# Feed-forward up projections with 512-column passes over both operand parts, one PSUM bank per output block

## The chip, the cores and the metric

The kernel runs on one core of one Trainium2 chip. The metric is the device time of one execution in microseconds (us); lower is better. TensorE does the matrix products, VectorE (DVE in the profile) and ScalarE (ACT) do the elementwise work, SyncE (SP) issues the loads, GpSimd (POOL) does almost nothing here.

## What is computed

Two layers of an encoder block over 256 tokens of 1024 features, all in float32. Each layer is a half-step feed-forward, a mixer (a state-space branch called S5, attention, and a convolution branch, gated and merged), and a second half-step feed-forward. The change touches the feed-forwards, of which there are four in all:

```python
D_MODEL, SEQ, DEPTH, D_FF = 1024, 256, 2, 2816

def rmsnorm(x, g):
    return x * lax.rsqrt(jnp.mean(x * x, axis=-1, keepdims=True) + EPS) * g

def swiglu_ffn(x, w_up, w_down):            # w_up: 1024 x 5632, w_down: 2816 x 1024
    a, b = jnp.split(x @ w_up, 2, axis=-1)
    return (jax.nn.silu(a) * b) @ w_down

def reference(...):
    for l in range(DEPTH):
        x = x + 0.5 * swiglu_ffn(rmsnorm(x, ffn1_norm[l]), ffn1_w_up[l], ffn1_w_down[l])
        ...                                  # mixer: w_in, three branches, gates, w_out
        x = x + 0.5 * swiglu_ffn(rmsnorm(x, ffn2_norm[l]), ffn2_w_up[l], ffn2_w_down[l])
    return x
```

## The kernel before

The residual stream is kept with features on partitions: `x[128, 8, 256]` is 8 blocks of 128 features by 256 tokens. A weight matrix is cut into 128x128 tiles, and `plan` fixes the order in which the tiles are used. Eight tiles make a chunk of 512 KB, which is one load (`fetch`, lines 318 to 341). For accuracy, each float32 operand is split into a high part and a remainder: for a chunk, ScalarE casts `raw` to `hi` (line 336) and VectorE subtracts to get `lo` (line 337). There are three `raw` and four `hi` and `lo` buffers. The activations are split in the same way, into `xh` and `xl`, which lie side by side in one tile `x2[128, 8, 2, 256]` (`norm_start`, `norm_block`). A product then needs three terms: hi·xh, hi·xl and lo·xh.

`prod` (lines 352 to 374) issues them in one of two forms. Where the operand is given as a pair `(xh, xl)`, a weight tile costs three matmuls of 256 columns, all summed into one 256-column area (lines 371 to 374). Where it is given as one tile that holds both parts, a weight tile costs one matmul of 512 columns, hi over (xh, xl), and one of 256 columns, lo over xh (lines 360 to 370); the two halves of the 512-column output are then added when they leave PSUM. In the kernel before, the down projections use the second form (their operand is `a2`, called AB in the profile) and the up projections and the mixer's projections use the first.

`ffn` (lines 464 to 520) is the feed-forward. The loop over `i` (22 steps) computes two output blocks, the a side and the b side, of 8 weight tiles each: 16 tiles a step. Both blocks of a step share one PSUM bank (line 482), except for the first steps. Then a chain leaves PSUM (lines 488 to 494): DVE multiplies the a side by the token factor `rb`, ACT takes a tanh, DVE multiplies twice (the second time by the b side, straight from PSUM), ACT casts the high part of `a2` and DVE subtracts the low part. After the loop, 8 down blocks of 22 weight tiles each follow; their evacuation `evac` copies one half of the bank with ACT, adds the other half with DVE, and updates `x`. A feed-forward thus has 352 up tiles and 176 down tiles; the four have 1408 up tiles. In the first feed-forward of a layer, `fill` holds the S5 branch's tables, small DVE and ACT work, recorded at the lowest priority (rank 4, line 496). The S5 tables of the second layer run mostly during the second feed-forward of the first layer, ahead of where the code records them.

The order of instructions on each engine is not the order of the code. `Recorder` records all operations with their dependencies, and `schedule` (lines 217 to 262) is a list scheduler that picks an order from rough costs of its own, given by `price` (lines 193 to 215): a float32r matmul of n columns is planned at n/2400 + 0.0025 us. `MARGIN` and `AUX_MARGIN` (0.3 and 0.8 us) are added before a matmul that depends on another engine. Each engine then executes its list strictly in that order, so an instruction that waits holds up all that is queued behind it. All recorded operations have line 268 in the profile, so the groups are told apart by tile names.

PSUM has 8 banks: `mm` has 3, `at` 2, and `y`, `pq` and `ax` 1 each (line 96). `pq` and `y` serve the S5 branch, `ax` the sums of the norms. Tiles of one tag take turns.

Of the kernel before, what the change touches and what calls it, by code (L numbers as in the profile page):

```python
"""Two layers of a parallel-branch encoder block (SwiGLU / S5 + attention + conv mixer / SwiGLU).

The residual stream is kept feature-major: x[feature on partitions, feature block, token].
Every large product runs on the tensor engine in float32r: both operands are split exactly
into a high part of 12 significant bits and the remainder, and three products carry the sum.
RMSNorm's 1/rms factor is per token and linear, so it is applied where a product leaves PSUM.
"""
# [20 lines left out]
EPS = 1e-6  # L28
NH, HD = 8, 64
CW = 31  # L30
U0, Q0, K0, V0, Z0, G0 = 0, 2, 6, 10, 14, 18     # 128-column blocks of w_in
CHT = 8                                            # weight tiles per DMA
MAGIC = 12582912.0                                 # 1.5 * 2**23: adding it rounds to integers
TWO_PI = 6.283185307179586
C1 = float(np.float32(6.28125))                    # 2*pi in three parts
# [13 lines left out]
GLU = 4                                            # blocks of the convolution's branch ahead of S5's GLU  # L49


def plan():
    out = []
    for l in range(L):
        for f in ("ffn1", "ffn2"):
            o = []
            if not out:
                o += [(f + "_w_up", k, c) for k in range(KD) for c in (0, KF, 1, KF + 1)]
            for i in range(2 if not out else 0, KF):
                o += _cols(f + "_w_up", KD, (i, KF + i))  # L60
            # the last operand block as late as possible
            o += _cols(f + "_w_down", KF - 1, (0, 1)) + [(f + "_w_down", KF - 1, c) for c in (0, 1)]
            o += _cols(f + "_w_down", KF, range(2, KD))
            if f == "ffn1":
                o += _cols("w_in", KD, (U0, U0 + 1, Z0, Z0 + 2, Z0 + 1, Z0 + 3))
                for c0 in (Q0, K0, V0):
                    o += [("w_in", k, c0 + c) for k in range(KD) for c in range(4)]
                o += _cols("w_in", KD, range(G0, G0 + 24))
                o += _cols("w_br_attn", 4, range(KD))
                o += _cols("w_br_conv", 2, range(GLU))  # L70
                o += _cols("s5_w_glu", 2, (0, 2, 1, 3))
                o += _cols("w_br_conv", 2, range(GLU, KD))
                o += _cols("w_br_s5", 2, range(KD))
                o += _cols("w_out", KD, range(KD))
            out += [(l,) + t for t in o]
    return out


NATIVE = ("w_br_conv", "s5_w_glu", "w_br_s5")      # few columns: float32 products, operands not split
# [15 lines left out]
TMP = dict(ev=4, th=3, sq=2, sa=2, sc=2, mc=4, s=2, pt=1, cv=2, jk=2)  # L95
# [4 lines left out]
#  # L100
# The program is first recorded in its logical order. Each engine runs its instructions in the order
# of issue, so that order is then chosen by a list scheduler with rough costs (they depend on shapes
# alone): the weight stream and what frees PSUM go first, the mixer's branches fill in.
# [23 lines left out]
class Recorder:  # L127
# [65 lines left out]
    def price(eng, name, outs, ins, kw):  # L193
# [5 lines left out]
        if eng == "pe":  # L199
            if name == "transpose":  # L200
                return 0.112, 0.2
            slow = kw["rhs"].dtype != F32R or n < 256
            rows = outs[0].partition_size()            # tiles of 32 or 64 columns run side by side
            return max(n / 2400.0 * (4 * rows / P if slow else 1) + 0.0025, 0.03), 0.2
# [12 lines left out]
    def schedule(self):  # L217
# [4 lines left out]
        wait = {e: [] for e in engs}       # (ready time, seq, op)  # L222
        can = {e: [] for e in engs}        # (rank, seq, op)
# [6 lines left out]
        while left:  # L230
# [11 lines left out]
            if soon:                       # a short chain that others wait for: no long one in between  # L242
                free[e] = min(soon)
                continue
# [26 lines left out]
# blocks of x that are loaded ahead of a part (chunk, column) of the weights  # L271
# [8 lines left out]
class Builder:  # L280
# [15 lines left out]
    # -- small helpers --  # L296
# [4 lines left out]
    # Tiles of one tag take turns in their slots, so work that runs at its own pace has its own tags.  # L301
# [15 lines left out]
    # -- weight stream --  # L317
# [33 lines left out]
    # -- products: out[feature, token] += w.T @ x --  # L351
    def prod(self, out, keys, ops, ks, start, stop):
        nc = self.nc
        for n, k in enumerate(ks):
# [5 lines left out]
            if not isinstance(ops, tuple):  # L360
                # one pass over both parts; the halves of out are added where it leaves PSUM
# [18 lines left out]
    def quad(self, outs, l, name, cs, ops, nk):  # L380
        """Output blocks that share every operand block as it arrives."""
        for k in range(nk):
            for o, c in zip(outs, cs):
                self.block(o, l, name, c, ops, nk, k, k + 1)

    def pair(self, outs, l, name, cs, ops, nk):
        """Two output blocks whose last operand block is used as late as possible."""
        for o, c in zip(outs, cs):
            self.block(o, l, name, c, ops, nk, 0, nk - 1)
        for o, c in zip(outs, cs):  # L390
            self.block(o, l, name, c, ops, nk, nk - 1, nk)

    # -- 1/sqrt on a small tile: bit-level seed and three Newton steps --
# [12 lines left out]
    def col_rsqrt(self, terms, inv_n, eps=EPS):  # L406
        """terms: [feature, token] tiles whose squares' sums over all features give the variance."""
# [10 lines left out]
    def spread(self, rc, out):  # L418
        """out[:, token] = rc[token] on every partition."""
# [9 lines left out]
    # -- RMSNorm: operands x*g split in two, 1/rms per token --  # L429
# [33 lines left out]
    # -- SwiGLU half step --  # L463
    def ffn(self, l, name, after=None, fill=()):
# [5 lines left out]
        ops = (self.xh, self.xl)  # L470
        pq = []
        for i in range(KF):
            if i == 0 and first:
                pq = [self.bank(t)[:, :T] for t in ("mm", "mm", "mm", "at")]
                self.quad(pq, l, up, (0, KF, 1, KF + 1), ops, KD)
                self.norm_end()
            elif i == 0:
                pq = [self.bank()[:, :T] for _ in range(2)]
                self.pair(pq, l, up, (0, KF), ops, KD)
                self.norm_end()  # L480
            elif not pq:
                ps = self.bank(("mm", "mm", "mm", "at", "at")[(i + 1) % 5])
                pq = [ps[:, :T], ps[:, T:]]
                for o, c in zip(pq, (i, KF + i)):
                    self.block(o, l, up, c, ops, KD)
            rb = self.rb
            t = self.tmp("ev")
            nc.vector.tensor_tensor(out=t, in0=pq.pop(0), in1=rb, op=ALU.mult)
# [3 lines left out]
            nc.vector.tensor_tensor(out=t, in0=t, in1=pq.pop(0), op=ALU.mult)  # L492
# [29 lines left out]
    # -- S5: decay and rotation tables --  # L522
# [23 lines left out]
    def s5_tables(self, l):  # L546
        """Returns a list of steps: cos/sin(theta*s) for every state and s, decay, and C times coef."""
# [7 lines left out]
        def small_part():  # L555
# [4 lines left out]
            # B, for products of split operands stacked along the contraction: rows (hi, hi, lo)  # L560
# [35 lines left out]
        def angle(j):  # L596
            # fraction of a turn in [-1/2, 1/2]
# [21 lines left out]
        def coefs():  # L619
# [17 lines left out]
            # C times coef, with the signs under which the four products of a state add up  # L637
# [16 lines left out]
    # -- mixer --  # L654
    def mixer(self, l, after):
# [6 lines left out]
        # u  # L662
# [12 lines left out]
        # S5 states, two groups (128 states) at a time  # L675
        y_ps = {}

        def s5_states(j):
            if j % 4 == 0:
                # channels of one state block on the same partitions, parts (hi, lo, hi) stacked  # L680
# [27 lines left out]
            # the products with sin take the place of this block's tables  # L708
# [19 lines left out]
        def s5_gelu(b):  # L728
            # gelu(y) (tanh form), doubled
# [12 lines left out]
        # conv: GLU with both halves of z  # L742
# [13 lines left out]
        # q, k, v with tokens on partitions  # L756
# [23 lines left out]
        # operands of the gates: normalised, in place  # L780
# [5 lines left out]
        # twice the convolution (hp holds twice the GLU): LayerNorm takes that out, with four times EPS  # L786
# [16 lines left out]
        def conv_norm():  # L803
# [17 lines left out]
            for q in range(2):  # L821
                # silu(v), doubled: v*(1 + tanh(v/2))
# [76 lines left out]
        # gates, with the branches' steps in between  # L899
# [19 lines left out]
        # branches' projections, gated and added  # L919
# [52 lines left out]
    def warm_up(self):  # L972
        """While the first loads are under way: the tensor engine's clock up, the Tanh table in."""
# [11 lines left out]
    def build(self):  # L985
        nc = self.nc
        # small parameters of the first layer and x come as one array
# [33 lines left out]
def layout(inputs):  # L1021
# [8 lines left out]
    sb = np.zeros((L, 3, 2, 16, 8, 2, 2, 64), np.float32)      # copy, g, ch | jb, re/im, g, state  # L1030
    for l in range(L):
# [19 lines left out]
        ct = np.zeros((2, 64, 8, 2, 2, 16), np.float32)        # g, state | jb, re/im, g, ch  # L1051
# [7 lines left out]
    # relative position bias per head, blocks (q 0..127, k 0..127) and (q 128..255, k 0..255);  # L1059
    # keys of later chunks are masked  # L1060
# [3 lines left out]
    full = inp["attn_rel_bias"][:, :, rel]                     # L, heads, q, k  # L1064
# [29 lines left out]
```

## Time and profile before

| what | value |
|---|---|
| time, median of 3 runs | 1187.76 us (1187.72 to 1188.9) |
| span of the profiled execution | 1186.6 us |
| PE (matmul) busy | 1177.4 us, 99% of the span |
| PEld (weight load) busy | 1097.8 us, 93% |
| DVE busy | 927.2 us, 78% |
| ACT busy | 645.6 us, 54% |
| DMA | 209.97 MB, mean 177 GB/s |
| granted TensorE clock | 1.000 |

The profiled execution's own time is its span, from the first to the last instruction; the median of the runs is 1.2 us above it. The profiler's records of matmuls overlap: a record lasts from the start of a matmul to its modelled end, and the next one starts earlier. Rates are therefore read from starts, not from durations. The same holds, to a lesser degree, for DVE and ACT.

### The profile page before, as it was taken

To read this page: it belongs to the slowest core of one execution; us is meant where nothing else is said; L and a number is where in the kernel's file an instruction comes from. 1 tells how busy PE (TensorE), PEld (TensorE's weight loads), DVE (VectorE), ACT (ScalarE), POOL (GpSimd) and SP (SyncE) were. 2 spreads that over 40 slices of the span, in tenths; PEclk is the share of its full clock that TensorE was granted. 3 is DMA by queue.
4 is the path that set the end of the run, shared out by engine and by line. 5 is a ranking of instruction groups with operands and counts; after the bars stand their busy time and mean duration, and the time that the engine had idled before them with its cause. 6 is when DMAs were issued, how large, how long until landed. Compare 5 with 4: busy or idle time off the path is not lost.

```text
span 1186.6 us, 21932 instructions
## 1 busy us (share of the span) xinstructions
PE 1177.4 (99%) x8565; PEld 1097.8 (93%) x8565; DVE 927.2 (78%) x1898; ACT 645.6 (54%) x1171; POOL 13.0 (1%) x32
## 2 busy tenths in 40 slices
PE   8999999999999999999999999999999999999998
PEld 7999989898888999998899999898987999999987
DVE  7999876998789998766676666779987888666654
ACT  6546554787643546645544444557875435444442
POOL 0000000000200000000000000000001000000000
PEclk9999999999999999999999999999999999999999
DMA  7655556554334565555555555565533435555552
GB/s 253 212 181 187 195 182 226 195 178 146 101 131 162 178 196 187 187 178 191 182 178 186 187 179 190 184 213 198 192 126 94 152 126 194 194 179 182 189 198 89
DMA packets 59751, 209.97 MB, mean 177 GB/s; under 512 B 6912, under 2 KB 9088, under 8 KB 59392
## 3 DMA queue, kind: packets, MB, share of 16 engines
q1 hardware_dynamic: 58496, 207.79, 50.9%
q8 instruction: 67, 1.10, 0.4%
q0 software_dynamic: 1152, 0.79, 0.3%
q14 instruction: 36, 0.29, 0.1%
HBM read 206.72 MB, written 1.05 MB: 175 GB/s over the span
## 4 chain that ended last, share of the span: by engine, by line
PE 98%; DMA 1%; DVE 0%; ACT 0%; SPq 0%; issue 0%; DVEq 0%
PE mm L268 72%; PE at L268 22%; PE ax L268 2%; PE y L268 1%; DMA px<-in_x 1%; PE pq L268 0%; SPq L268 0%; DVE x L268 0%; DVE acc L268 0%; ACT sq L268 0%; DVE lo L268 0%; DVE ev L268 0%; ACT x L268 0%; DVE px L268 0%; ACT ev L268 0%
## 5 line engine op out<-in xcount | busy, mean ns | idle before, releaser
L268 ACT CAST hi<-raw 128x1024 fp32r<-128x1024 f32 (+1 forms) x373 | 389.8, 1047 | 406.8 <-issue 166.7
L268 DVE TENSOR_TENSOR lo<-raw,hi 128x1024 fp32r<-128x1024 f32 (+1 forms) x373 | 454.9, 1221 | 165.7 <-ACT hi L268 161.9
L268 PE MATMUL mm<-x,hi 128*128 128x256 f32 x2736 | 505.8, 284 | 1.9 <-ACT hi L268 1.8
L268 PEld LDWEIGHTS mm<-x,hi 128*128 128x128 f32 x2736 | 424.5, 189 | 11.4 <-issue 7.4
L268 PE MATMUL mm<-x,lo 128*128 128x256 f32 x1368 | 388.3, 285 | 0.4 <-DVE lo L268 0.2
L268 PEld LDWEIGHTS mm<-x,lo 128*128 128x128 f32 x1368 | 257.2, 188 | 4.7 <-issue 3.8
L268 PE MATMUL mm<-AB,hi 128*128 128x512 f32 x704 | 246.6, 398 | 0.0
L268 PE MATMUL mm<-AB,lo 128*128 128x256 f32 x704 | 193.1, 281 | 0.0
L268 PE MATMUL at<-x,hi 128*128 128x256 f32 x1040 | 188.6, 282 | 0.1
L268 PEld LDWEIGHTS at<-x,hi 128*128 128x128 f32 x1040 | 160.6, 189 | 0.3 <-ACT hi L268 0.3
L268 PEld LDWEIGHTS mm<-AB,hi 128*128 128x128 f32 x704 | 130.6, 188 | 29.7
L268 PE MATMUL at<-x,lo 128*128 128x256 f32 x520 | 146.6, 282 | 0.0
L268 PEld LDWEIGHTS mm<-AB,lo 128*128 128x128 f32 x704 | 132.9, 189 | 2.6
L268 PEld LDWEIGHTS at<-x,lo 128*128 128x128 f32 x520 | 97.9, 188 | 0.0
L268 PE MATMUL mm<-tbl,hi 128*128 128x256 f32 x256 | 46.3, 284 | 0.0
L268 PE MATMUL at<-hi,x 128*128 128x512 f32 x128 | 41.0, 396 | 0.0
L268 PEld LDWEIGHTS mm<-tbl,hi 128*128 128x128 f32 x256 | 39.9, 192 | 0.3 <-ACT tbl L268 0.3
L268 ACT ACTIVATE th<-ev 128x256 f32<-128x256 f32 x88 | 36.2, 412 | 7.2 <-DVE ev L268 7.0
L268 ACT CAST AB<-ev 128x256 fp32r<-128x256 f32 x88 | 34.9, 400 | 6.5 <-DVE ev L268 6.2
L268 DVE SCALAR_TENSOR_TENSOR ev<-th,ev 128x256 f32<-128x256 f32 x88 | 36.8, 419 | 1.2 <-ACT th L268 1.2
L268 DVE TENSOR_TENSOR AB<-ev,AB 128x256 fp32r<-128x256 f32 x88 | 36.6, 419 | 0.4 <-ACT AB L268 0.2
L268 DVE TENSOR_TENSOR ev<-mm,rb 128x256 f32<-128x256 f32 x56 | 23.6, 424 | 15.6 <-PE mm L268 13.5
(222 smaller groups left out, 1174.1 us busy)
## 6 DMA issues: line engine op xcount, KB each, us to landing
raw<-in_w SPq DMA_DIRECT2D x371, 512.0 KB, 3.7
lo<-in_w SPq DMA_DIRECT2D x10, 512.0 KB, 4.4
AB<-in_b SPq DMA_DIRECT2D x2, 1536.0 KB, 7.9
mc<-in_s SPq DMA_DIRECT2D x8, 192.0 KB, 4.1
out_x<-px SPq DMA_DIRECT2D x8, 128.0 KB, 3.2
raw<-in_w SPq DMA_DIRECT2D x2, 256.0 KB, 3.8
px<-in_x SPq DMA_DIRECT2D x1, 512.0 KB, 7.7
ct<-in_p SPq DMA_DIRECT2D x2, 256.0 KB, 3.7
```

What stands on the lines that cost most here:

```text
L268: fn(*args, **kw)
```

## The change

The up projections now hand `self.x2` to `prod` in place of the pair `(xh, xl)`, so each of their weight tiles takes the second form: one matmul of 512 columns and one of 256. Each output block now fills a whole bank, so a step of the loop takes two banks. The banks are drawn in turn from seven, `mm`, `at`, `pq` and `y`. Each block's two halves are added on leaving PSUM, by a ScalarE copy of the second half and a VectorE addition of the first, before the chain goes on from SBUF. The pool `ev` has 5 buffers in place of 4. The planner's cost of a float32r matmul of 256 columns or more is now n/2240 + 0.006 us, for the whole program. The rest of the diff removes comments.

```diff
-TMP = dict(ev=4, th=3, sq=2, sa=2, sc=2, mc=4, s=2, pt=1, cv=2, jk=2)
+TMP = dict(ev=5, th=3, sq=2, sa=2, sc=2, mc=4, s=2, pt=1, cv=2, jk=2)
...
-            slow = kw["rhs"].dtype != F32R or n < 256
-            rows = outs[0].partition_size()            # tiles of 32 or 64 columns run side by side
-            return max(n / 2400.0 * (4 * rows / P if slow else 1) + 0.0025, 0.03), 0.2
+            rows = outs[0].partition_size()
+            if kw["rhs"].dtype != F32R or n < 256:
+                return max(n / 2400.0 * 4 * rows / P + 0.0025, 0.03), 0.2
+            return n / 2240.0 + 0.006, 0.2
...
-        ops = (self.xh, self.xl)
+        turn = iter(("mm", "mm", "mm", "at", "at", "pq", "y") * KF)
         pq = []
         for i in range(KF):
             if i == 0 and first:
-                pq = [self.bank(t)[:, :T] for t in ("mm", "mm", "mm", "at")]
-                self.quad(pq, l, up, (0, KF, 1, KF + 1), ops, KD)
+                pq = [self.bank(next(turn)) for _ in range(4)]
+                self.quad(pq, l, up, (0, KF, 1, KF + 1), self.x2, KD)
                 self.norm_end()
             elif i == 0:
-                pq = [self.bank()[:, :T] for _ in range(2)]
-                self.pair(pq, l, up, (0, KF), ops, KD)
+                pq = [self.bank(next(turn)) for _ in range(2)]
+                self.pair(pq, l, up, (0, KF), self.x2, KD)
                 self.norm_end()
             elif not pq:
-                ps = self.bank(("mm", "mm", "mm", "at", "at")[(i + 1) % 5])
-                pq = [ps[:, :T], ps[:, T:]]
+                pq = [self.bank(next(turn)) for _ in range(2)]
                 for o, c in zip(pq, (i, KF + i)):
-                    self.block(o, l, up, c, ops, KD)
+                    self.block(o, l, up, c, self.x2, KD)
             rb = self.rb
-            t = self.tmp("ev")
-            nc.vector.tensor_tensor(out=t, in0=pq.pop(0), in1=rb, op=ALU.mult)
+            t, u = self.tmp("ev"), self.tmp("ev")
+            for v in (t, u):
+                ps = pq.pop(0)
+                nc.scalar.copy(out=v, in_=ps[:, T:])
+                nc.vector.tensor_tensor(out=v, in0=ps[:, :T], in1=v, op=ALU.add)
+            nc.vector.tensor_tensor(out=t, in0=t, in1=rb, op=ALU.mult)
             th = self.tmp("th")
             nc.scalar.activation(out=th, in_=t, func=AF.Tanh, scale=0.5)
             nc.vector.scalar_tensor_tensor(out=t, in0=th, scalar=1.0, in1=t, op0=ALU.add, op1=ALU.mult)
-            nc.vector.tensor_tensor(out=t, in0=t, in1=pq.pop(0), op=ALU.mult)
+            nc.vector.tensor_tensor(out=t, in0=t, in1=u, op=ALU.mult)
```

## Rows read from the trace of the kernel before

**Rows 1.** Waits of PE on other engines, whole span (total us, times, longest).
```profile
PE mm L979 <- ACT iota L975: 2.3, 1, 2.3
PE mm L268 <- ACT hi L268: 1.8, 1, 1.8
PE mm L268 <- DVE lo L268: 0.2, 1, 0.2
```

**Rows 2.** Chain of work in order of time, last up projection (start us, us, what).
```profile
1004.64 11.52 PE at L268 x96
1016.16 17.28 PE mm L268 x144
...
1091.04 11.52 PE at L268 x96
```

**Rows 3.** Timeline of PE, first and last matmul of the last down projection.
```profile
1119.68 0.39 PE L268 MATMUL mm<-AB,hi 128*128 128x512 f32 x1
...
1181.62 0.39 PE L268 MATMUL mm<-AB,hi 128*128 128x512 f32 x1
```

**Rows 4.** Chain of work, 48 matmuls of 512 columns in the mixer.
```profile
229.18 11.25 PE mm L268 x48
```

**Rows 5.** Busy us by stretch: first up, first down, second up, last up, last down, first mixer.
```profile
core 0: us, PE busy (x) PEld busy (x) DVE busy (x) ACT busy (x) POOL busy (x), PEclk, DMA share, GB/s
33.75:137.43 103.68, 103.68 (x865) 103.68 (x865) 95.26 (x248) 59.54 (x81) 0.00 (x0) 1.00 0.58 194
137.43:199.60 62.17, 62.17 (x354) 53.94 (x354) 45.92 (x103) 31.18 (x45) 0.00 (x0) 1.00 0.54 190
418.72:533.76 115.04, 115.04 (x961) 115.04 (x960) 95.13 (x189) 64.03 (x87) 0.00 (x0) 1.00 0.54 185
1004.64:1119.68 115.04, 115.04 (x962) 115.04 (x960) 80.36 (x123) 54.82 (x81) 0.00 (x0) 1.00 0.54 185
1119.68:1181.62 61.94, 61.94 (x353) 53.74 (x352) 32.74 (x44) 22.95 (x28) 0.00 (x0) 1.00 0.46 160
205.94:410.51 204.57, 204.57 (x1435) 182.62 (x1436) 181.60 (x406) 128.19 (x308) 5.96 (x12) 1.00 0.46 157
```

**Rows 6.** Timeline of PE at the start: first waits for the weights.
```profile
11.23 0.98 PE L268 MATMUL mm<-x,hi 128*128 128x256 f32 x6 [1.80 <-ACT hi L268]
...
15.98 0.63 PE L268 MATMUL mm<-x,lo 128*128 128x256 f32 x3 [0.22 <-DVE lo L268]
```

**Rows 7.** Timeline of DVE in the first up projection, instructions back to back.
```profile
104.10 1.22 DVE L268 TENSOR_TENSOR lo<-raw,hi 128x1024 fp32r<-128x1024 f32 x1
105.24 0.42 DVE L268 SCALAR_TENSOR_TENSOR ev<-th,ev 128x256 f32<-128x256 f32 x1
105.57 0.42 DVE L268 SCALAR_TENSOR_TENSOR tbl<-tbl,mc 128x256 f32<-128x256 f32 x1
105.91 0.42 DVE L268 TENSOR_TENSOR ev<-ev,mm 128x256 f32<-128x256 f32 x1
```

**Rows 8.** Groups by shape, the evacuation of the down blocks (count, busy us, mean ns).
```profile
L268 ACT COPY ev<-mm 128x256 f32<-128x256 f32 x32 | 11.8, 371 | 30.0 <-PE mm L268 29.5
L268 DVE TENSOR_TENSOR ev<-mm,ev 128x256 f32<-128x256 f32 x32 | 13.1, 420 | 16.5 <-ACT ev L268 16.5
```

**Rows 9.** Tile pq: first use of the S5 tables, at 281.7 us.
```profile
L268 DVE TENSOR_TENSOR sa<-pq,tbl x16: 664/683/692, 281.7 to 931.8; 128x512 f32<-128x512 f32 x16
```

**Rows 10.** Timeline of ACT in the first up projection: the casts of the weights.
```profile
105.71 1.05 ACT L268 CAST hi<-raw 128x1024 fp32r<-128x1024 f32 x1 [1.51 <-PE mm L268]
108.59 1.05 ACT L268 CAST hi<-raw 128x1024 fp32r<-128x1024 f32 x1 [1.53 <-PE mm L268]
```

**Rows 11.** Timeline of ACT in the first mixer: two heads' transposed blocks.
```profile
306.18 0.49 ACT L268 ACTIVATE pt<-at 128x384 f32<-128x384 f32 x1 [2.03 <-PE at L268]
...
311.10 0.49 ACT L268 ACTIVATE pt<-at 128x384 f32<-128x384 f32 x1 [1.02 <-PE at L268]
```

**Rows 12.** Waits in the first mixer, 205 to 410 us: attention's ACT work behind PE.
```profile
ACT pt L268 <- PE at L268: 4.6, 5, 2.0
ACT nat L268 <- PE ax L268: 5.4, 3, 2.7
```

## The prediction

> **What bounds the kernel now.** I read the waits of PE first. Over the whole span PE waited 1.8 us for a cast and 0.2 us for a remainder, and once 2.3 us for the warm-up's table [rows 1]. So PE's own list sets the time, and a microsecond taken from that list is a microsecond of the span as long as the other engines keep ahead.
>
> Next comes the rate of PE in each stage, read from the chain of work, since there the pieces are cut at starts. The up projections run without a break: 96 matmuls in 11.52 us, 144 in 17.28 us, and so on up to the last piece at 1091.04 [rows 2]. That is 0.1200 us a matmul and 0.3600 us a weight tile of three. The down projections already have the form that the change brings to the up projections. In the last one, the first matmul starts at 1119.68 and the last at 1181.62 [rows 3]. With one 512-column matmul after that (11.25 / 48 = 0.2344 us [rows 4]), 176 tiles take 62.17 us, which is 0.3533 us a tile. Both forms pass 768 columns a tile, so the new form gains only what a matmul costs beside its columns. The granted clock is 1.00, the 2.4 GHz level, in all these stretches [rows 5], so the two rates may be compared.
>
> Last I read how much room DVE and ACT have. In the last up projection DVE is busy 80.36 us of 115.04 and ACT 54.82; in the first one, where the S5 tables are made beside the products, DVE is busy 95.26 of 103.68 [rows 5]. The change adds work just there.
>
> **The change, part by part.** *The matmuls.* All 1408 up tiles change form. The first 32, at the start, wait for the weights' casts (1.80 and 0.22 us [rows 6]) and not for PE's rate, so I count nothing for them. The bounds there are 32 x 0.0067 = 0.2 us gained and one DVE pass of 0.42 us [rows 7] lost, because the first 512-column pass needs xl as well as xh. The other 1376 gain 0.3600 - 0.3533 = 0.0067 us each, 9.2 us. The lower bound comes from the mixer's 512-column matmuls: two of 0.1200 replaced by one of 0.2344 [rows 4] gain 0.0056 a tile, 7.7 us. I take 9.2, because the down projections have the very instructions, order and weights' stream that the up projections will have.
>
> By the rows, a saved matmul is thus worth 5.6 to 6.7 ns. The Trainium skill (TensorE: Matmul & The Clock Gate, section "Wait — 56ns, not 53.3ns?") puts the fixed cost of a warm matmul at about 2.5 ns. By that the sum would be an estimated 1376 x 0.0025 = 3.4 us and not 9.2. The trace disagrees: 256 columns take 0.1200 here and 512 take 0.2344.
>
> *The additions on leaving PSUM.* Each step of the loop gains two ACT copies and two DVE additions. The down blocks' evacuation has both, at 0.371 and 0.420 us [rows 8]. Over 88 steps that is 176 x 0.371 = 65 us on ACT and 176 x 0.420 = 74 us on DVE, all beside the products if it fits. In a stretch with no tables, 115.04 us is 20 steps of 5.76 us; DVE needs 80.36 / 20 = 4.02 us a step, and 4.86 with the additions, of the new step of 16 x 0.3533 = 5.65 us. ACT goes from 2.74 to 3.48. Both fit, so this costs nothing in the second layer.
>
> With the tables it is close. In the stretch of the first up projection (18 steps) DVE's work beyond 18 x 4.02 is 22.8 us. With the additions the sum of durations is 18 x 4.86 + 22.8 = 110.3 us, against 18 x 5.65 = 101.8, which is 8.5 us too much. But durations overstate a full engine: back to back, a remainder starts its successor after 1.14 us (not 1.22) and a 256-column operation after 0.33 to 0.34 (not 0.42) [rows 7]. By starts the base is 2 x 1.14 + 6 x 0.34 = 4.32 us a step, and the sum is 100.6: it just fits. What doesn't fit can go into the down projection behind it, where DVE idles 62.17 - 45.92 = 16 us [rows 5], and the tables are first read at 281.7 us [rows 9], long after. The second up projection needs 20 x 4.86 + 14.8 = 112 us of 113 even by durations. So I take 0, with bounds of 0 and 8.5 us. I choose 0 because a full engine is nearer to the back-to-back rows.
>
> What covers this: a cast of `hi` waits for PE to release a buffer, every 2.88 us [rows 10], so a chunk is cast when the fourth chunk ahead of it has been used. Its remainder is ready 1.05 + 1.22 us after that, and it is needed three chunks later, 3 x 2.83 = 8.5 us. DVE may therefore fall behind by about 6.2 us before PE notices. Without that cover every microsecond of DVE's lag would be PE's.
>
> *The waits that are added.* An ACT copy now waits for a block's last matmul, with the next cast of weights queued behind it on ACT; the DVE addition waits for the copy, with the next remainder behind it. The plan places both after the block's planned end, so the waits should be short; each that is longer than planned eats into the 6.2 us of cover, and only beyond that costs PE anything. No DMA is added or moved; SP's loads hang on the remainders as before. POOL is untouched.
>
> *PSUM.* Two banks a step out of seven come round again after 3.5 steps, 19.8 us, and a block needs a copy and an addition, about 0.8 us, to free its bank. The a side can now leave while the b side is computed. At the end of an up projection the last chain is about eight passes of 0.4 us, 3.3 us, while the first two down blocks cover 42 x 0.3533 = 14.8 us before they need its result.
>
> *The new price.* The planner's 256-column matmul goes from 0.1092 to 0.1203 us, a tile of the mixer from 0.3275 to 0.3608 (the chip: 0.3600). Nothing in the mixers' work changes, but their order is planned anew. PE is busy in all of the first mixer's 204.57 us [rows 5], so I see no gain there and take 0; the loss has a rival below.
>
> The sum is made against the profiled execution: 1186.6 - 9.2 = 1177.4 us. The median of the runs is 1.2 us above its span, so the forecast is 1178.6 us, 0.8% faster.
>
> **The rivals.** *DVE becomes the pace while the tables are made.* If the durations are the true cost, DVE is 8.5 us short in the first up projection, and PE sees between 8.5 - 6.2 = 2.3 us (all of the cover used) and 8.5 us (none). Time: 1180.9 to 1187.1. For it: 95.26 us busy of 103.68 already. Against it: the back-to-back starts, and a planner that counts 0.34 us for such an operation, as the chip does, and so knows about the shortage.
>
> *The plan loses its cushion: slower.* Today the chip takes 10% longer for a tile than the plan thinks, so PE comes to each attention step later than planned, about 0.5 us over the 4.9 us from one head's transposed block to the next [rows 11]. Results from DVE and ACT are there by then. With the true price this is gone, and each PE instruction that needs a short chain has only the planned margin. There are three such steps a head (scores, transposes, product with v), 48 in the two mixers, and some 34 more for S5, the convolution and the norms. The gain of 9.2 us is eaten at 9.2 / 82 = 0.11 us a step. If the 48 steps of attention lose half of the cushion, it costs 48 x 0.25 = 12 us: 1190.6 us. For it: the plan's latencies are rough, and so far nothing has tested them. Against it: ACT waits for PE here and not PE for ACT, 0.9 us on average before a transposed block is copied (4.6 us over 5 waits) and 1.8 us after a head pair (5.4 over 3) [rows 12], which is more than the cushion that goes.
>
> *The saving is only a small fixed cost.* If the down projections' rate owes something to what doesn't carry over, the gain is a third to a half of mine, 3.4 us: 1184.4 us. The two rates agree against it [rows 3, 4].
>
> *The weight loads are the pace.* PEld is busy in all of the up stretch and in 53.74 of 61.94 us of the down stretch [rows 5]. If up tiles went by their loads (0.36 / 3 each), two loads would be 0.24 us, and the span would fall by up to 1376 x 0.12 = 165 us; but the down tile with its two loads takes 0.3533, so the columns would stop it at once. The Trainium skill (Perfetto Trace Analysis, section "Identifying the Most-Contended Engine") takes the busy share of weight loads as the better gauge of TensorE; here that share falls from 100% to 87% between two stages that run at nearly the same rate.
>
> *It changes nothing.* DVE and the plan's gaps give back just what PE gains: within 0.2%, 2.4 us, of before, which is about what a measurement of this kernel can tell from no change.
>
> **How the numbers follow.** The forecast (7.7 to 10 us gained: 1177.8 to 1180.1) gets 0.66. DVE as the pace gets 0.14, of which 0.03 lies within 0.2%. Slower through the plan gets 0.09, the small fixed cost 0.03, the loads 0.01 and no change 0.03. A plan that also closes small gaps in the mixers (1176 to 1177) gets 0.04. Faster: 0.66 + 0.11 + 0.03 + 0.01 + 0.04 = 0.85. Same: 0.06. Slower: 0.09. The range runs from 1176.0 to 1185.5: it takes in the forecast, the better half of DVE's rival, the small fixed cost and the tidier plan, somewhat over 8 in 10.
>
> **What would show it.** Right: up tiles at 0.353 us in the chain, with two matmuls a tile (some 113 in 20 us); PE's waits still near 2 us; DVE about 86% busy in the last up projection; casts of `hi` still waiting for PE. DVE as the pace: PE waiting for `lo` in the first up projection. The lost cushion: PE waiting for ACT or DVE in the mixers, and a mixer longer than 204.6 us. The prediction is wrong if up tiles don't reach 0.353 us where nothing waits.

## The result, and the profile after

The changed kernel takes 1175.97 us (median; 1175.09 to 1177.18) against 1187.74 us before: ratio 0.9899 [0.9885, 0.9913]. The forecast was 1178.6 us, so the direction was right and the size was not: 11.8 us gained instead of 9.2, just past the low end of the range. The spans of the profiled executions, 1173.3 and 1186.6 us, lie 13.3 us apart, 1.5 us more than the medians, in part because the profiled execution of after was the fastest of its four (1175.09 us). All stages below are read from these two executions.

The page of the changed kernel, its span and the busy time of the engines:

```profile
span 1173.3 us, 19674 instructions
PE 1165.3 (99%) x7157; PEld 1021.8 (87%) x7157; DVE 983.5 (84%) x2074; ACT 700.5 (60%) x1347; POOL 13.0 (1%) x32
```

Its waits of PE, whole span (total us, times, longest), to be set beside [rows 1]:

```profile
PE mm L984 <- ACT iota L980: 2.3, 1, 2.3
PE pq L269 <- ACT us L269: 0.4, 1, 0.4
PE mm L269 <- ACT hi L269: 0.2, 1, 0.2
PE at L269 <- ACT nat L269: 0.2, 1, 0.2
```

PE still bounds the kernel. The two new waits, behind `us` and `nat`, sum to 0.6 us. The start's wait for a cast fell from 1.8 to 0.2 us.

The chain of work in the last up projection (start us, us, what), beside [rows 2]:

```profile
991.77 5.62 PE at L269 x32
997.40 2.81 PE pq L269 x16
1000.20 2.81 PE y L269 x16
1003.01 8.42 PE mm L269 x48
...
1090.02 5.61 PE at L269 x32
```

Two matmuls are a weight tile now, so 8.42 / 24 = 0.3508 us a tile. It was 0.3600, and the forecast was 0.3533.

The timeline of PE, first and last 512-column matmul of the last down projection, beside [rows 3]:

```profile
1106.69 0.40 PE L269 MATMUL mm<-AB,hi 128*128 128x512 f32 x1
...
1168.36 0.39 PE L269 MATMUL mm<-AB,hi 128*128 128x512 f32 x1
```

From first start to last end this stage takes 61.67 + 0.23 = 61.90 us, 0.3517 us a tile, with nothing in it changed by the diff; before it took 62.17.

Busy us by stretch, in the order of [rows 5] (first up, first down, second up, last up, last down, first mixer):

```profile
core 0: us, PE busy (x) PEld busy (x) DVE busy (x) ACT busy (x) POOL busy (x), PEclk, DMA share, GB/s
31.88:132.74 100.86, 100.86 (x577) 87.88 (x577) 99.59 (x251) 64.02 (x113) 0.00 (x0) 1.00 0.59 193
132.74:194.64 61.90, 61.90 (x353) 53.91 (x352) 53.41 (x147) 35.06 (x49) 0.00 (x0) 1.00 0.64 200
411.79:526.71 114.92, 114.92 (x657) 100.11 (x656) 107.82 (x229) 78.08 (x131) 0.00 (x0) 1.00 0.61 193
991.77:1106.69 114.92, 114.92 (x657) 100.14 (x656) 99.77 (x169) 71.68 (x125) 0.00 (x0) 1.00 0.59 192
1106.69:1168.36 61.67, 61.67 (x352) 53.71 (x351) 32.78 (x45) 23.02 (x28) 0.00 (x0) 1.00 0.49 161
200.54:406.92 206.38, 205.85 (x1431) 183.42 (x1432) 182.42 (x414) 129.27 (x309) 5.96 (x12) 1.00 0.50 159
```

The windows of the last row, here and in [rows 5], start about 6 us into the first mixer and end over 4 us behind it, so they are not the mixer's length; the table below has that. In the first up projection DVE is busy 99.59 of 100.86 us, and PE doesn't pause. The granted clock is 1.00 in every stretch, as before, so it explains no difference. Cut at PE's first matmul of each stage (behind a mixer, at that mixer's last matmul), the 13.3 us are:

| stage, us | before | after | difference |
|---|---|---|---|
| start and first up | 137.26 | 132.74 | -4.52 |
| other up projections (each) | 127.70, 127.57, 127.71 | 124.53, 124.38, 124.53 | -9.54 together |
| down projections (each) | 62.19, 61.90, 61.89, 62.17 | 61.90, 61.90, 61.90, 61.90 | -0.55 |
| mixers | 206.61, 206.85 | 207.54, 207.27 | +1.35 |

So three things differ from the forecast: an up tile gains 3.17 / 352 = 0.0090 us and not 0.0067, the start gives over 1 us more than its tiles' rate explains, and the mixers get longer.

### The profile page after: what moved, and what is told of

It reads as the page before. It is cut to its first block, busy times and chain, and to the rows that moved or that the text cites. A ratio compares the mean times of both kernels' runs of the same rounds, so it can differ in the third digit from the quotient of the medians.

```text
span 1173.3 us, 19674 instructions
## 1 busy us (share of the span) xinstructions
PE 1165.3 (99%) x7157; PEld 1021.8 (87%) x7157; DVE 983.5 (84%) x2074; ACT 700.5 (60%) x1347; POOL 13.0 (1%) x32
## 4 chain that ended last, share of the span: by engine, by line
PE 97%; DVE 1%; DMA 0%; ACT 0%; issue 0%; SPq 0%; DVEq 0%
PE mm L269 64%; PE at L269 18%; PE y L269 7%; PE pq L269 6%; PE ax L269 2%; DVE lo L269 1%; DMA px<-in_x 0%; DVE acc L269 0%; DVE ev L269 0%; ACT nat L269 0%; DVE x L269 0%; DVE nt L269 0%; SPq L269 0%; DVE y L269 0%; DVE gl L269 0%
## 5 line engine op out<-in xcount | busy, mean ns | idle before, releaser
L269 PE MATMUL mm<-x,hi 128*128 128x256 f32 (+1 forms) x1600 | 408.9, 331 | 0.3 <-ACT hi L269 0.2
L269 PE MATMUL mm<-x,lo 128*128 128x256 f32 x1120 | 304.4, 284 | 0.3
L269 PEld LDWEIGHTS mm<-x,hi 128*128 128x128 f32 x1600 | 268.1, 189 | 31.0 <-issue 6.9
L269 PEld LDWEIGHTS mm<-x,lo 128*128 128x128 f32 x1120 | 210.1, 188 | 11.0 <-issue 2.7
L269 PE MATMUL at<-x,hi 128*128 128x512 f32 x384 | 135.6, 394 | 0.0
L269 PEld LDWEIGHTS at<-x,hi 128*128 128x128 f32 x384 | 70.6, 188 | 13.0
L269 PE MATMUL pq<-x,hi 128*128 128x512 f32 x192 | 69.4, 394 | 0.0
L269 PE MATMUL y<-x,hi 128*128 128x512 f32 x192 | 69.4, 394 | 0.0
L269 PE MATMUL pq<-x,lo 128*128 128x256 f32 x192 | 49.8, 279 | 0.0
L269 PE MATMUL y<-x,lo 128*128 128x256 f32 x192 | 49.8, 279 | 0.0
```

Of the source, the lines that this page charges most:

```text
L269: fn(*args, **kw)
```

## The experiments

The question is why an up tile came out at 0.3508 us when a down tile of the same form, beside it, takes 0.3517 to 0.3533. The first theory kept the prediction's idea, a fixed cost per matmul, with some luck in each stage. The rival was that PE's rate hangs on where the operands lie in SBUF: `x2` and `AB` are different tiles, and both forms read `x2`. A tool for that is a pad, an unused tile that moves what is allocated after it and changes no instruction. Below, "distance" is the start address of the moving operand less that of the weights `hi`, modulo 128 bytes. In before and after, `x2` starts at byte 28928 of a partition, `AB` at 94624 and the first of the four `hi` buffers at 61856 (the others 4096 bytes apart), so `x2` lies at distance 96 and `AB` at 0. `raw` and `lo` have `hi`'s place modulo 128 in every run, and `tbl` and the temporaries `ev` have that of `AB`.

**The change again.** The same kernel a second time, to see what repeats.

> The changed kernel once more, unaltered, beside the next three on one chip. In the profiled execution of before the third load of x landed 6.10 us after its issue, and the start-up ended 1.3 us later than in after. Theory 'chance of one execution': the start-up's length follows that load's landing and differs between executions of one kernel; this run's up projection starts within 1.3 us of after's and its time is 1175 to 1177 us. Rival: the change itself shortens the start-up; then the first down projection starts at 132.7 us again whenever x lands.

1175.71 us, 0.9899 [0.9886, 0.9913]. Every stage came out within 0.2 us of the table above. The stage times are therefore properties of the kernel, and differences of 0.5 us in a stage can be read, or smaller ones that all four projections show.

**Before again.**

> The kernel before once more, unaltered, for a second profile. The start-up of the changed kernel was the same in two executions (first down projection at 132.74 and 132.57 us), though the loads of x landed at different times. Theory 'chance of one execution': in before the third load of x landed late in the profiled execution only; in this one the first down projection starts near 136.0 us in place of 137.26, that is, 1.3 us earlier, and the span shrinks by as much. Rival 'the change shortens the start-up': 137.3 us again.

1187.78 us, span 1186.0. The first up projection ended at 136.96 us, not at 136.0. Its first down projection took 61.90 us where the other execution had 62.19, so at distance 0 that stage has two levels in one and the same kernel. What held up the start was again a load, another one this time. Its chain of work has this piece (start us, us, what):

```profile
16.25 6.37 DMA raw<-in_w
```

The chain of the first execution of before has a load of the input, also long:

```profile
2.60 6.10 DMA px<-in_x
```

The chain of after has the same load, shorter:

```profile
1.66 4.47 DMA px<-in_x
```

Late loads at the start (6.10 and 6.37 us, against 4.47 after) go with the 1 us that the first stage gained beyond its rate. Both executions of before had one on this chain and neither of after did, but the first stage of the next kernel, with before's form, ended at 136.28. Whether the change causes the difference stays open.

**The price alone, in the kernel before.**

```
-            slow = kw["rhs"].dtype != F32R or n < 256
...
-            return max(n / 2400.0 * (4 * rows / P if slow else 1) + 0.0025, 0.03), 0.2
+            if kw["rhs"].dtype != F32R or n < 256:
+                return max(n / 2400.0 * 4 * rows / P + 0.0025, 0.03), 0.2
+            return n / 2240.0 + 0.006, 0.2
```

> The kernel before with only the planner's new price of a matmul (n/2240 + 0.006 us); no matmul and no elementwise operation changes. After showed the up tiles 1.3 us earlier at the end of the start-up and the two mixers together 1.35 us longer. Theory 'the re-plan': the new order is what moves both. Then the up tiles stay at 0.360 us, the mixers take 0.4 to 0.9 us more each, and the whole is 0 to 1.4 us slower than before (1187.7 to 1189.2 us). Rival 'the form': the mixers' loss comes from the fuller DVE and ACT queues that the evacuations leave behind; then this run agrees with before within 0.5 us.

1189.5 us, 1.0014 [1.0006, 1.0023]: slower by 0.1%. Up tiles stayed at 0.3600; the mixers took 207.03 and 208.60 us, 0.4 and 1.75 more, the second beyond what was expected. None of PE's listed waits lies in a mixer.

**The change with the old price.** The lines marked - above put back in the kernel after.

> The changed kernel with the planner's old price (n/2400 + 0.0025 us); the 512-column passes, banks and additions stay. Theory 'the re-plan': up tiles at 0.351 us as in after, the mixers back at their length of before, so 1.35 us faster than after, 1174.6 us. Rival of the prediction 'the plan's cushion': with the old price the cushion is back, so any wait of PE in the mixers of after is gone. Rival 'DVE as the pace': the old plan thinks PE 9% faster and DVE just as fast, so it may put too much work on DVE while the S5 tables are made; then PE waits for the weights' remainders in the first up projection, by up to 8.5 us.

1174.48 us, 0.9887 [0.9875, 0.9900]. The mixers are at 206.96 and 206.85 us, 1.0 less than in after together, the waits behind `us` and `nat` are gone, PE never waits for `lo`, and the up projections stand at 124.5. So the new form and the new price are separate: the form gives the gain, and the price takes 1 to 2 us of it back in the mixers.

**DVE given more.** One more pass of DVE on each of the 176 evacuated blocks, a maximum of the block with itself.

```
                 nc.vector.tensor_tensor(out=v, in0=ps[:, :T], in1=v, op=ALU.add)
+                nc.vector.tensor_tensor(out=v, in0=v, in1=v, op=ALU.max)
```

> The changed kernel with one more DVE pass of 256 columns on each block that leaves PSUM (the maximum of a tile with itself, so the values stay): two passes more a step. Theory 'a full DVE costs start to start': 4.32 + 0.68 = 5.0 us of DVE a step of 5.61, and with the tables 1.27 more, 6.3; the planner knows the cost and moves the tables towards the down projections, so the time grows by 0 to 3 us over the changed kernel. Rival 'durations are the cost': 4.86 + 0.84 = 5.70 us a step already without tables; PE waits for the remainders in all four up projections, 22 x 0.1 us in each of the last two and 15 us or more in the first, 15 to 25 us in all.

1178.67 us, 3.0 more than the change. The first up projection ends 2.0 us later, the first mixer is 1.1 us longer, and the other up projections stay at 124.5. PE's waits for `lo`, whole span:

```profile
PE mm L269 <- DVE lo L269: 1.4, 2, 1.1
```

Both lie in the first 31 us, at the start, where a load of weights took 6.65 us. Busy us in the first up projection and in 109 us of the last one (columns as in the stretches above):

```profile
31.90:134.72 102.82, 102.76 (x587) 89.18 (x586) 102.28 (x243) 63.87 (x113) 0.00 (x0) 1.00 0.58 194
1000.00:1109.00 109.00, 109.00 (x623) 94.98 (x622) 105.16 (x198) 64.54 (x118) 0.00 (x0) 1.00 0.58 192
```

The first up projection says little on the price of a pass: the planner moved the tables out of it. The first pass that writes `tbl` starts at 134.4 us, where after has it at 74.2, and DVE made 243 passes in place of 251, though 36 were added. The last up projection, without tables, does show the price. By count times mean duration its 198 passes add up to 115.2 us; they ran in 109.00 us, with DVE busy 105.16, and PE lost nothing. The back-to-back starts [rows 7] are thus the better price for a full DVE.

**`AB` moved by 96 bytes** (distance 0 to 96), in the kernel after.

```
         self.iota = self.const.tile([P, T], F32, name="iota")
+        self.big.tile([P, 24], F32, name="pad")
```

> The changed kernel with an unused tile of 96 bytes per partition ahead of the down projections' operand AB; nothing else changes, in order or work. In after a tile takes 0.3509 us in the up projections and 0.3533 in the down projections, though both are one 512-column and one 256-column matmul; x2, the up operand, starts at byte 28928 of a partition, a multiple of 256, and AB at 94624, which is 32 above a multiple of 64. The pad puts AB at 94720, a multiple of 256. Theory 'the start address of the moving operand': the down tiles fall to 0.351 us, 704 x 0.0024 = 1.7 us faster than after, 1174.3 us. Rival 'the stage' (22 tiles summed in one bank in place of 8, other work beside them): the down tiles stay at 0.3533 us and the time at 1176.0.

1174.79 us, 0.9888 [0.9876, 0.9901]. All four down projections took 61.65 or 61.66 us, 0.3503 a tile, where after has 61.90; the first mixer lost 1.2 us. The same instructions on the same data run at another rate: the fixed-cost theory has no place for that.

**`x2`, `hi` and `AB` moved** by 32, 64 and 64 bytes (`x2` to distance 64, `AB` still at 0).

```
+        self.res.tile([P, 8], F32, name="pad0")
         self.norm_start("g1", 0)
+        self.res.tile([P, 8], F32, name="pad1")
```

> The changed kernel with the up projections' operand x2 shifted by 32 bytes per partition (an unused 32-byte tile ahead of it and another behind, so that what follows keeps its place relative to 64 bytes). Theory 'the start address of the moving operand': the up tiles go from 0.3509 to 0.3533 us, the rate that the prediction had used, 1376 x 0.0024 = 3.3 us slower than after (1179.3 us); the other products from x2 slow down by a little too; the down tiles stay at 0.3533. Rival 'the stage': nothing changes, 1176.0 us.

1173.58 us, 0.9877 [0.9864, 0.9890], where 1179.3 was expected: a miss. I had taken the operands' own alignment for the cause. The up projections became 0.1 to 0.2 us shorter, the mixers 1.0 and 1.6. The timeline of PE in the last up projection shows the tiles alternate:

```profile
1067.67 0.39 PE L269 MATMUL at<-x,hi 128*128 128x512 f32 x1
1068.02 0.40 PE L269 MATMUL at<-x,hi 128*128 128x512 f32 x1
1068.37 0.40 PE L269 MATMUL at<-x,hi 128*128 128x512 f32 x1
1068.73 0.39 PE L269 MATMUL at<-x,hi 128*128 128x512 f32 x1
1069.08 0.40 PE L269 MATMUL at<-x,hi 128*128 128x512 f32 x1
1069.43 0.40 PE L269 MATMUL at<-x,hi 128*128 128x512 f32 x1
```

The starts are 0.35 us apart, once 0.36; over the stage the mean is 0.3503.

**The same shift with the old price.** The edits above together.

> The changed kernel with both x2 shifted by 32 bytes and the planner's old price. Theory 'the two are independent': the old price gives back what the new plan cost in the mixers (about 1.5 us) and the shift its own 2 us; 1172 us, with both mixers below 206.5 us. Rival: what the shifted kernel gained in the mixers was the chance of another interleaving and not the address of x2; then this run is like the changed kernel with the old price alone, 1174.5 us.

1171.52 us, 0.9862 [0.9848, 0.9875]. By the medians price and address add up, as expected. The stages show it less well: the first mixer took 206.68 us and not under 206.5, and both mixers together are only 0.3 us shorter than with the shift alone.

**All on multiples of 128 bytes, `hi` too** (both distances 0).

```
         self.norm_start("g1", 0)
+        self.res.tile([P, 24], F32, name="pad")
```

> The changed kernel with 96 unused bytes behind x2, so that x2, the weights' parts hi and lo, AB and the mixer's operands all start at multiples of 256 bytes. So far x2 was at such a multiple and hi and lo at 32 above a multiple of 64. Theory 'the moving operand's own address': up tiles 0.351 us and down tiles 0.350 us as with AB alone aligned, about 1174.8 us. Rival 'the address relative to the weights': the tile rates depend on how the moving operand lies against the weight being loaded; with both at multiples of 256 the up tiles change, to 0.346 or 0.354 us, that is 1408 x 0.005 = 7 us faster or 4 us slower.

1178.56 us, 0.9919 [0.9906, 0.9933]: slower than the change. Its chain of work at the end:

```profile
1084.67 8.46 PE mm L269 x48
...
1104.42 67.83 PE mm L269 x384
```

The up tile rises to 8.46 / 24 = 0.3525 us. The last piece holds 16 up and 176 down tiles and gives 67.83 / 192 = 0.3533. Aligned operands are the slowest, so own alignment falls. What the moves have in common is the distance to the weights: at 0, either operand gives 0.352 to 0.353.

**`AB` at distance 32.** The shifted kernel with the old price, and a pad of 32 bytes more ahead of `AB`.

```
+        self.big.tile([P, 8], F32, name="pad2")
```

> The changed kernel with the old price, x2 shifted by 32 bytes, and AB moved by 32 bytes more, so that AB starts at a multiple of 64 while hi and lo start 32 above one. Theory 'the address relative to the weights': the down tiles take 0.350 us again as with AB alone aligned (61.65 us a stage and not 62.04), 4 x 0.39 = 1.6 us less than the shifted kernel with the old price: 1169.9 us. Rival 'the moving operand's own address' gives the same here; the next run tells them apart.

1166.63 us, 0.9822 [0.9808, 0.9837]; 1169.9 was expected. The down projections took 61.14 us, 0.3474 a tile, against 62.04 without the pad. The unexpected part came from two places: the down projections fell below the 61.65 us expected (0.5 us each), and the mixers fell from 206.68 and 205.25 us to 204.78 and 204.80. The weights stayed where they were, so their own place isn't the cause either.

**Distances of before, mirrored** (`x2` at 96, `AB` at 32, new price).

```
+        self.res.tile([P, 8], F32, name="pad0")
+        self.big.tile([P, 8], F32, name="pad2")
         self.norm_start("g1", 0)
```

> The changed kernel with x2 and AB at 32 above a multiple of 64 and hi and lo at a multiple of 64: the mirror image of the run in which AB alone was moved. Theory 'the address relative to the weights': operand and weights lie 32 bytes apart within 64 again, so up tiles take 0.351 us and down tiles 0.350 us (61.65 us a stage). Rival 'the moving operand's own address': an operand at 32 above a multiple of 64 takes 0.353 us or alternates, as AB does in after; the down stages take 61.9 to 62.2 us. Rival 'multiples of 256 for the weights are slow in themselves': up tiles at 0.353 us as with all of them aligned.

1171.75 us, 0.9864 [0.9847, 0.9880]. The chain of work at the end:

```profile
1087.18 5.61 PE at L269 x32
...
1098.40 66.76 PE mm L269 x384
```

5.61 / 16 = 0.3506 a tile for `x2`, the rate of after at the same distance but at other addresses. The last piece less 16 such tiles leaves 61.15 us, 0.3474, for `AB`, the rate of the kernel above.

**Both at distance 32**, the change with the old price.

```
+        self.big.tile([P, 8], F32, name="pad2")
         self.norm_start("g1", 0)
+        self.res.tile([P, 16], F32, name="pad1")
```

> The changed kernel with the planner's old price and with unused tiles that put x2 and AB at multiples of 128 bytes and hi and lo at 96 above one, so that the moving operand starts 32 bytes after the weights, modulo 128, in both projections. So far, by that distance: 0 gave 0.352 to 0.353 us a tile, 96 gave 0.350 to 0.351, 32 gave 0.3474. Theory 'the distance modulo 128 sets the rate': up tiles at 0.347 us too, about 123.1 us an up stage in place of 124.35, so 4 x 1.2 = 4.8 us less than the run with AB alone at that distance: 1161.8 us. Rival 'x2 is at its floor': up tiles stay at 0.350 to 0.351 us and the time at 1166.6 us or a little above.

1164.04 us (1163.52 to 1165.22), 0.9798 [0.9784, 0.9812], the fastest here. The chain of work at the end:

```profile
1071.38 8.38 PE mm L268 x48
1079.76 5.59 PE at L268 x32
...
1090.93 66.75 PE mm L268 x384
```

`AB` does as expected, 0.3474. `x2` reaches 8.38 / 24 = 0.3492, not the 0.347 that I expected: distance isn't all of it.

**The kernel before with the same pads.** Three matmuls of 256 columns a tile, nothing of the change. This one sizes the change itself.

> The kernel before with the same unused tiles: three matmuls of 256 columns a tile in the up projections, old price, x2 and AB 32 bytes after the weights modulo 128. Theory 'the distance acts on every pass': the up tiles fall below 0.360 us, by about as much as the mixer's output projection, which has the same form, fell (22.48 in place of 23.10 us for 64 tiles, 0.0097 us a tile), so by some 13 us, and the down stages to 61.14 us: 1170 us. Rival 'only the 512-column pass feels it': up tiles stay at 0.360 us, and only the down stages and the mixers gain, about 6 us: 1182 us.

1165.93 us (1165.27 to 1167.04), 0.9816 [0.9802, 0.9830], where 1170 was expected; the mixers, too, became 2.6 and 2.7 us shorter. The chain of work, one piece of the second up projection and the end:

```profile
421.87 16.96 PE mm L268 x144
...
1053.60 16.80 PE mm L268 x144
1070.40 11.20 PE at L268 x96
1081.60 77.95 PE mm L268 x496
```

The old form goes from 17.28 to 16.80 us for 144 matmuls, 0.3600 to 0.3500 us a tile, in three of the four up projections. The second one goes at 16.96 / 48 = 0.3533 all along, with `x2` at the same place, so distance alone doesn't fix the rate. Without any edit of the products, two pads gain 21.5 us, nearly twice what the change did. With both operands at distance 32, the change is worth 0.3500 - 0.3492 = 0.0008 us a tile, and 1165.93 - 1164.04 = 1.9 us in all, of which that one projection accounts for 352 x 0.0033 = 1.2.

## Why the prediction was right, and where it failed

*The bound.* Right. PE's list sets the time before and after, and what was taken from an up tile left the span.

*The matmuls: the step that failed.* The term 1376 x (0.3600 - 0.3533) = 9.2 us was too small: the chain gives 1376 x (0.3600 - 0.3508) = 12.7. The prediction took the rate from the down projection because it had "the very instructions, order and weights' stream". It hadn't the same operand: `AB` lies at distance 0, `x2` at 96, and the runs with pads moved each rate alone. The stage chosen was also one of the two slower of four (62.17, where two others took 61.90, 0.3517 a tile); the other two would have given 1376 x 0.0083 = 11.4 us. The lower bound [rows 4] had the same fault, another operand's rate.

*What a saved matmul is worth.* The reading behind it fell too. 5.6 to 6.7 ns were not a matmul's fixed cost: with both operands at distance 32 a matmul less saves 0.8 ns. Most of the gain is that at distance 96 the old form loses 0.3600 - 0.3500 = 0.0100 us a tile against distance 32, and the new form only 0.3508 - 0.3492 = 0.0016. The rival "only a small fixed cost" was thus nearer on the mechanism and further off on the time. By the 2.5 ns of the Trainium skill (TensorE: Matmul & The Clock Gate, section "Wait — 56ns, not 53.3ns?") the gain is an estimated 3.4 us. The measured 1.9 us at distance 32 lies nearer to that than to 9.2, and the 11.8 us of the change is outside of what that rule covers.

*The additions.* Right: hidden, at the end of the bounds that was chosen. DVE was busy 99.59 of 100.86 us in the first up projection with no wait of PE for `lo`, and what didn't fit went into the down projection, where DVE rose from 45.92 [rows 5] to 53.41 us. The run with one more pass bears out the price, start to start and not by durations; it doesn't measure the 6.2 us of cover, since PE never waited for `lo` past the start. (The 22.8 us of other DVE work is 22.9 by the prediction's own rows, which changes nothing.) The rival "DVE becomes the pace" needed the durations.

*The added waits and PSUM.* Right at 0: no wait of PE for a bank or for an evacuation stands among PE's waits.

*The new price.* Taken as 0, and wrong: the mixers became 1.35 us longer, of which the old price gives back 1.0; as the only edit it cost 2.2 us in the mixers and 2.0 in the whole kernel. The rival "the plan loses its cushion" has its place and its sign right, not its size: 48 steps at 0.25 us were 12 us. Its mechanism is borne out only in part. PE's waits in the mixers of after name 0.6 us (`us`, `nat`), and they go with the old price; with the price alone PE has no listed wait there at all. The rest is the order of work and was not followed further.

*The start.* Taken as 0 with bounds of -0.2 and +0.4; it gave more than 1 us. The first stage gained 4.52 us and its rate explains 3.2. Late loads in before's executions account for that only in part. The start's and the down projections' gains and the mixers' loss nearly cancel, so it is luck that the spans' 13.3 us lie near the matmuls' 12.7.

*The weight loads.* Refuted, as argued: 0.3508 us a tile with PEld at 87%.

*The signs named beforehand.* "A mixer longer than 204.6 us" was no sign: 204.6 us was the length of a window in [rows 5], and before's first mixer takes 206.61. DVE at 99.77 of 114.92 (87%) in the last up projection, foreseen as about 86%; PE's waits at 3.1 us, foreseen near 2.

## What to carry to other kernels

A rate that is borrowed from another stage needs the same operand as well as the same instruction: read it in every stage that has the form, and take a spread among them as a sign of something unseen. Before a product's form is changed to save a per cent, pad the tiles that feed it and time that, because where the operands lie was worth 21.5 us here and the form 1.9. When an engine is nearly full, price it by the starts of back-to-back rows, since summed durations call it overfull too soon.

## What the runs showed of the hardware

At the granted clock of 1.00 the rate of PE depended on the distance between the start addresses of the moving operand and of the weights, modulo 128 bytes (float32r, us for a weight tile of 768 columns):

| distance | 3 matmuls of 256 columns | 512 + 256 columns |
|---|---|---|
| 0 | 0.361 (`w_out`, 23.1 us / 64 tiles) | 0.3517 to 0.3533 |
| 32 | 0.3500 (`x2`; one projection 0.3533), 0.351 (`w_out`) | 0.3474 (`AB`), 0.3492 (`x2`) |
| 64 | 0.353 (`x2` in the mixers) | 0.3503 (`x2`, alternating) |
| 96 | 0.3600 (`x2`) | 0.3503 (`AB`), 0.3508 (`x2`) |

The old form at 64 stands in the mixers of the run with `x2`, `hi` and `AB` moved, where the products from `x2` still take three matmuls; 12.49 x 3 / 106 = 0.353 us a tile:

```profile
254.11 12.49 PE mm L269 x106
```

Moved together by equal amounts, operand and weights kept the slow rate; moved apart, they changed it. That the distance matters is shown by these runs; what in the chip does it is not. Nor is the period: all pads were multiples of 32 bytes, and every distance run is 0 to 96 modulo 256 as well. Since `raw` and `lo` move with `hi`, it stays open whose accesses meet the operand's. The place of `AB` and the temporaries is not it for `x2`, which kept 0.3506 to 0.3508 at distance 96 with `AB` at 0, 32 and 96. Open, too, is why `AB` and `x2` differ at 32, why one projection of four ran at 0.3533 there, and why `AB` at distance 0 runs at 0.346 us a tile for a while (five tiles from 1107.05 to 1108.78 in after) in a stage whose mean is 0.3517. Each pad also moved tiles that weren't read here, and the mixers, which read `x2` and `tbl`, answered by up to 2.7 us (206.85 to 204.13, both with the old price).
